# Scores of a pair of attention heads: full-row products replaced by half-row products, and all small-tile products of a pair in one run

## The chip, the cores and the metric

The program runs on one core of one Trainium2 chip. The core has five engines that work through their instructions in program order, each on its own: PE (TensorE, matrix products, with its weight loads shown apart as PEld), DVE (VectorE), ACT (ScalarE), POOL (GpSimd) and SP (SyncE, which here only issues DMA loads). They wait for one another through semaphores. Products are written to PSUM, which has eight banks; everything else lies in SBUF. The metric is the device time of one execution in microseconds (us).

## The reference

Two decoder layers on one sequence of 256 tokens with 1024 features. Layer 0 mixes tokens by dilated attention in 16 heads of 64 features, layer 1 by gated linear attention (GLA) in chunks of 64; each is followed by a gated ConvFFN. Shift, scale and gate of each sub-layer come from a vector c (`silu(c) @ w_ada`). The change is in the dilated attention:

```python
A_CONFIGS = ((128, 1), (512, 4), (2048, 16))       # (window, dilation), three groups g
qkv = (h @ w_in).reshape(B, S, A_GROUPS, 3, A_HEADS, A_HEAD_DIM)
for g, (window, dilation) in enumerate(A_CONFIGS):
    o, lse = dilated_branch(q[g] * scale, k[g], v[g], rel_bias[...], window, dilation)
# in a branch: query t attends keys t - j*dilation, j = 0..window/dilation
s = einsum('bnqrhe,bnkrhe->bnrhqk', qb, kk) + bias
s = where(mask, s, NEG_INF)
p = exp(s - max(s)); den = sum(p); o = p @ v / den; lse = max(s) + log(den)
# the three groups are mixed by their shares
wts = softmax(stack(lses), axis=0)
o = sum(wts[..., None] * stack(outs), axis=0)
y = o.reshape(B, S, A_WIDTH) @ w_out
```

Mixing three softmaxes by their log sums is one softmax over the keys of all three groups. The kernel works in that form: for each query one row of scores, 256 columns for group 0 (the "shared" scores: all tokens are possible keys) and 64 columns each for groups 1 and 2 (the "dilated" ones: only keys of the query's own residue modulo 4).

## The kernel before

**Products and weights.** Every large product is made in three passes of fp32r from a high and a low part of each operand (`mm3`, lines 175 to 177). `split` (L155) loads a piece of a weight on SP's queue into a slot `raw` (L159), ACT rounds it to `whi` (L165, two halves) and DVE subtracts to get `wlo` (L169, two halves). The slots `raw`, four of them, are shared with the pieces of `w_ada`, which `ada_chunk` loads (L133); DVE takes two products with c from each (L138) and ACT adds a bias (L146, L148). `next_ada()` is called once behind each of the three evacuations of a pair, and its load takes a `raw` slot too.

**Pairs of heads.** The attention works through eight pairs of heads, u = 0 to 7. For a pair, three pieces of 1 MB give q and k of the three groups (48 products each of 256 columns into a bank `pqk`), and two pieces of 0.75 MB give v (48 products of 384 columns into two banks `pv`). Pairs 0 and 1 get q and k from weights loaded at the very start. `evacuate` (L474 on) takes q and k out of PSUM: for groups 1 and 2 q on ACT (L479) and k on DVE (L480); for group 0 high and low parts of both, q into tiles in which the two heads stand on different rows with zeros elsewhere (L484, L485, written for each head apart), k (L489, L490). `by_group` (L494 on) copies v out: for the first 128 tokens on ACT (L497 to L500), for the second on DVE (L497, L498) and ACT (L499, L500). `pqk` and `pv` share two banks (tag `p`), so a pair's first pqk product has to wait until v of the pair before is copied.

**Scores.** `attend` goes over the four residues r of the query position. `shared` makes three products with all 128 rows of the array, where the zeros in q keep the heads apart: 64 queries of one head and 64 of the other in one tile (L417). `dilated` adds four products of 64x64 in two quadrants of the array (L424, two instructions of PE each). DVE adds the bias and takes the maximum (L435), ACT makes the exponentials (L444) with DVE's negated maximum (L441), DVE normalizes (L450, L451) to `pn`, PE transposes (L455), ACT or DVE copies to `pt` (L456), and the outputs are products with v (L460, L464) into a bank `po`, taken out at L469 and L470. The relative bias is a tile that is loaded from DRAM by four small DMAs a pair (L345, L346), once the loads issued before it stand in the queue.

**What sets the order.** Each engine runs in the order in which a scheduler has written out its instructions; it is fixed at build time, and it follows the pools (how many banks and slots there are) and `behind(...)`, which says that an instruction must stand after another on its engine. The banks have three tags: `p` 2, `s` 3, `t` 3. After the attention, `project` makes the output projection with w_out.

Of the kernel before, what the change touches and what calls it, by code (L numbers as in the profile page):

```python
# [18 lines left out]
P = 128  # L19
D = 1024  # L20
T = 256
# [36 lines left out]
def trunk(ctx: ExitStack, tc: tile.TileContext, I, out):  # L58
# [275 lines left out]
    shift(att, 32)  # L334
    rows = att.tile([16, NROW], F32, tag="pt", name="rows")

    def load_bias(u):

        b = att.tile([P, KEYS + 3], F32, tag="bias", name="bias")
        r = rows_d[:, :]
        for hh in range(2):
            own, at = slice(CH * hh, CH * hh + CH), r.offset + (2 * u + hh) * NROW
            nc.sync.dma_start(b[own, 2 * CH :], bass.AP(r.tensor, at, [[4, CH], [1, T + 3]]))  # L345
            nc.sync.dma_start(b[own, 0 : 2 * CH].rearrange("p (g x) -> p g x", g=2),  # L346
                              bass.AP(r.tensor, at + 512, [[1, CH], [P, 2], [1, CH]]))
        return b[:, :]
# [19 lines left out]
    with behind(norm_ops[0]):  # L368
        keep_warm(3)
        for i, (g, n) in enumerate(ROWS):  # L370
            c = slice(at, at + n)
            ps = bank("rows", "t")[:16, 0:n]
# [33 lines left out]
    def attend(u, q, k, v, bias):  # L406
# [3 lines left out]
        prob = [att.tile([P, KEYS + 3], F32, tag="prob", name="prob", bufs=6) for _ in range(4)]  # L410
        pt = att.tile([P, 4, KEYS], F32, tag="pt", name="pt")
        heads = [slice(E * hh, E * hh + E) for hh in range(2)]

        def shared(s, r):
            n = T + r + r % 2
            for i, (a, b) in enumerate(((0, 0), (1, 0), (0, 1))):
                mm(s[:, 0:n], q[0][a][:, r].rearrange("p a b -> p (a b)"), k[0][b][:, 0:n], start=(i == 0), stop=(i == 2))  # L417

        def dilated(s, r):
            own = slice(CH * r, CH * r + CH)  # L420
            for g in (1, 2):
                at = T + r + CH * (g - 1)
                for e in heads:
                    mm(s[e, at : at + CH], q[g][e, own], k[g][e, own], start=True, stop=True)  # L424

        for h in range(2):
            s = [bank("s", "s") for _ in range(2)]
            shared(s[0], 2 * h)
            dilated(s[0], 2 * h)
            shared(s[1], 2 * h + 1)  # L430
            dilated(s[1], 2 * h + 1)
            for i in range(2):
                r = 2 * h + i
                back = bass.AP(bias.tensor, bias.offset + KEYS - 1 + r, [bias.ap[0], [-1, KEYS + r]])
                nc.vector.tensor_tensor_reduce(  # L435
                    prob[r][:, 0 : KEYS + r], s[i][:, 0 : KEYS + r], back,
                    op0=ALU.add, op1=ALU.max, scale=1.0, scalar=-3e38, accum_out=m[:, r : r + 1],
                )
        for h in range(2):
            rs = slice(2 * h, 2 * h + 2)  # L440
            nc.vector.tensor_scalar(m[:, 4:8][:, rs], m[:, 0:4][:, rs], -1.0, None, op0=ALU.mult)  # L441
            for r in (2 * h, 2 * h + 1):
                c = prob[r][:, 0 : KEYS + r]
                nc.scalar.activation(c, c, AF.Exp, bias=m[:, 4 + r : 5 + r], accum_out=m[:, 8 + r : 9 + r])  # L444
            nc.vector.reciprocal(m[:, 12:16][:, rs], m[:, 8:12][:, rs])
            for r in (2 * h, 2 * h + 1):

                f = m[:, 12 + r : 13 + r]
                pn = att.tile([P, KEYS], F32, tag="pn", name="pn", bufs=3)
                nc.vector.tensor_scalar(grouped(pn[:, 0:T]), by_residue(prob[r][:, 0:T]), f, None, op0=ALU.mult)  # L450
                nc.vector.tensor_scalar(pn[:, T:KEYS], prob[r][:, T + r : KEYS + r], f, None, op0=ALU.mult)  # L451
# [4 lines left out]
                (nc.vector.tensor_copy if r % 2 else nc.scalar.copy)(pt[:, r, :], t[:, 0:KEYS])  # L456
        po = bank("po", "t")
        for n in range(2):
            for hh, e in enumerate(heads):
                mm(grouped(po[e, :T]), v[n][:, e], pt[:, :, P * n + E * hh : P * n + E * hh + E], start=(n == 0), stop=False)  # L460
        for r in range(4):
            for hh, e in enumerate(heads):
                at = P * (r % 2) + P + E * hh
                mm(po[e, CH * r : CH * r + CH], v[r // 2][:, at : at + E],  # L464
                   pt[:, r, T + E * hh : T + E * hh + E], start=False, stop=(r == 3))
# [8 lines left out]
    def evacuate(q, k, g, pq, pk):  # L474
# [7 lines left out]
        for hh in range(2):  # L482
            own = slice(E * hh, E * hh + E)
            nc.scalar.mul(qh[own, :, hh, :], grouped(pq[own]), 0.125)  # L484
            nc.vector.scalar_tensor_tensor(ql[own, :, hh, :], grouped(pq[own]), 0.125, qh[own, :, hh, :].bitcast(F32),  # L485
                                           op0=ALU.mult, op1=ALU.subtract)
# [15 lines left out]
    q_pair = [[att.tile([P, 4, 2, CH], F32R, tag=f"q0{i}{j}", name="q", bufs=1) for j in range(2)] for i in range(2)]  # L502
    for z in q_pair[0] + q_pair[1]:
# [576 lines left out]
```

## Time and profile before

| what | value |
|---|---|
| time of three runs | 786.73, 784.63, 786.98 us; median 786.73 |
| span of the profiled execution | 783.8 us |
| the profiled execution's own time | only the span is given; it lies 2.9 us below the median |
| PE, DVE, ACT, POOL busy | 771.8, 643.3, 481.6, 14.3 us |
| read from HBM | 182.59 MB, mean 236 GB/s by all queues |

The page gives for each engine the time in which it had an instruction running, and for a group of like instructions its line, engine, operation, output and inputs, how many, the busy time, the mean of one in ns, and the idle time of the engine just before with what ended it. In the timeline a row has start, duration, engine, line, operation, tiles, and how many; records of PE overlap, since products are pipelined. Times there are from the start of the span. The windows view gives the busy time of each engine in a stretch. SPq rows are DMA issues on SP's queue; a DMA's landing time is counted from its issue.

### The profile page before, as it was taken

Reading aid. Unit: us, or ns where it says so; the run is one execution under the profiler, and the core shown is the slowest. Engines: PE = TensorE matmul, PEld = TensorE weight load, DVE = VectorE, ACT = ScalarE, POOL = GpSimd, SP = SyncE. Lnnn points to the kernel's source line nnn. Section 1 sums busy time; section 2 is a strip of 40 time slices with the busy share of each in tenths; the row PEclk is TensorE's granted clock in tenths of the full one; section 3 lists DMA queues with packets and bytes.
Section 4 is the critical chain, followed back from the end, with each engine's and each line's share of the span. In section 5 each row is a group of like instructions: output and inputs, shape, how many; then the busy total and the mean of one; then the engine's idle time right before and its main releaser. Section 6 shows DMA issues by size and latency. Waiting matters only on the chain.

```text
span 783.8 us, 15888 instructions
## 1 busy us (share of the span) xinstructions
PE 771.8 (98%) x6416; PEld 743.3 (95%) x6416; DVE 643.3 (82%) x1160; ACT 481.6 (61%) x940; POOL 14.3 (2%) x40
## 2 busy tenths in 40 slices
PE   8999999999999999999999999999999999999997
PEld 5999989999999999999999999898999999999997
DVE  6998979878788758999998886797567898899762
ACT  5566555545545557866666655665667866667552
POOL 1000000000000010000000000000010000000000
PEclk9999999999999999999999999999999999999999
DMA  9998577595775726777645994966445765555651
GB/s 350 405 313 350 192 306 256 205 320 195 268 289 198 273 92 249 255 265 268 222 147 196 314 331 178 337 240 231 146 139 186 256 206 176 210 180 211 220 198 54
DMA packets 32616, 184.72 MB, mean 236 GB/s; under 512 B 5852, under 2 KB 7388, under 8 KB 16286
## 3 DMA queue, kind: packets, MB, share of 16 engines
q1 hardware_dynamic: 32160, 183.26, 65.6%
q8 instruction: 50, 0.82, 0.4%
q10 hardware_dynamic: 382, 0.45, 0.2%
q14 instruction: 24, 0.20, 0.1%
HBM read 182.59 MB, written 1.10 MB: 234 GB/s over the span
## 4 chain that ended last, share of the span: by engine, by line
PE 75%; DVE 12%; DMA 8%; ACT 3%; issue 2%; ACTq 0%; DVEq 0%
PE pab L176 10%; PE pab L177 10%; PE pab L175 10%; PE pd L175 5%; PE pd L176 5%; PE pd L177 5%; DVE wlo L169 5%; DMA raw<-in_wqk 4%; PE pqk L177 3%; PE pqk L176 3%; PE pqk L175 3%; DVE ada_raw L138 2%; PE py L175 2%; PE py L176 2%; DMA raw<-in_wv 2%; PE py L177 2%
## 5 line engine op out<-in xcount | busy, mean ns | idle before, releaser
L169 DVE TENSOR_TENSOR wlo<-raw,whi 128x1024 fp32r<-128x1024 f32 (+3 forms) x274 | 291.7, 1096 | 53.1 <-ACT whi L165 52.4
L165 ACT CAST whi<-raw 128x1024 fp32r<-128x1024 f32 (+3 forms) x274 | 245.5, 945 | 130.3 <-PE pab L176 40.6
L177 PE MATMUL pab<-hhi,wlo 128*128 128x256 f32 x672 | 184.7, 276 | 0.0
L176 PE MATMUL pab<-hlo,whi 128*128 128x256 f32 x672 | 184.6, 276 | 0.0
L175 PE MATMUL pab<-hhi,whi 128*128 128x256 f32 x672 | 183.2, 277 | 0.0
L176 PEld LDWEIGHTS pab<-hlo,whi 128*128 128x128 f32 x672 | 126.0, 188 | 0.2
L177 PEld LDWEIGHTS pab<-hhi,wlo 128*128 128x128 f32 x672 | 126.1, 188 | 0.0
L175 PEld LDWEIGHTS pab<-hhi,whi 128*128 128x128 f32 x672 | 125.1, 188 | 0.1
L138 DVE CUSTOM_DVE_ANT_0 ada_raw<-ada_raw,c_bc 128x1024 f32<-128x1024 f32 x96 | 113.4, 1218 | 12.4 <-DMA ada_raw<-in_w_ada 12.4
L176 PE MATMUL pqk<-hlo,whi 128*128 128x256 f32 x440 | 123.0, 284 | 0.3 <-DVE hlo L260 0.3
L177 PE MATMUL pqk<-hhi,wlo 128*128 128x256 f32 x440 | 122.4, 283 | 0.0
L175 PE MATMUL pqk<-hhi,whi 128*128 128x256 f32 x440 | 120.8, 286 | 0.5 <-ACT v L500 0.5
L177 PE MATMUL pd<-ghi,wlo 128*128 128x256 f32 x352 | 97.1, 276 | 0.0
L176 PE MATMUL pd<-glo,whi 128*128 128x256 f32 x352 | 97.1, 276 | 0.0
L175 PE MATMUL pd<-ghi,whi 128*128 128x256 f32 x352 | 96.8, 276 | 0.0
L176 PEld LDWEIGHTS pqk<-hlo,whi 128*128 128x128 f32 x440 | 83.6, 190 | 1.0 <-DVE hlo L260 0.5
L177 PEld LDWEIGHTS pqk<-hhi,wlo 128*128 128x128 f32 x440 | 83.2, 190 | 0.9 <-issue 0.7
L175 PEld LDWEIGHTS pqk<-hhi,whi 128*128 128x128 f32 x440 | 82.1, 191 | 1.7 <-ACT v L500 0.6
L176 PEld LDWEIGHTS pd<-glo,whi 128*128 128x128 f32 x352 | 66.1, 188 | 0.0
L177 PEld LDWEIGHTS pd<-ghi,wlo 128*128 128x128 f32 x352 | 66.1, 188 | 0.0
L175 PEld LDWEIGHTS pd<-ghi,whi 128*128 128x128 f32 x352 | 65.9, 188 | 0.0
L641 ACT ACTIVATE r<-pab,small 128x256 f32<-128x256 f32 x86 | 46.7, 559 | 15.5 <-DVE r L644 15.4
(215 smaller groups left out, 1307.2 us busy)
## 6 DMA issues: line engine op xcount, KB each, us to landing
ada_raw<-in_w_ada SPq DMA_DIRECT2D x47, 1024.0 KB, 6.6
raw<-in_w_up SPq DMA_DIRECT2D x42, 1024.0 KB, 5.0
raw<-in_w_down SPq DMA_DIRECT2D x32, 704.0 KB, 5.1
raw<-in_wqk SPq DMA_DIRECT2D x18, 1024.0 KB, 7.0
raw<-in_wv SPq DMA_DIRECT2D x14, 768.0 KB, 4.5
raw<-in_w SPq DMA_DIRECT2D x7, 960.0 KB, 6.5
raw<-in_w_out_a SPq DMA_DIRECT2D x4, 1024.0 KB, 6.2
raw<-in_w_v_b SPq DMA_DIRECT2D x4, 1024.0 KB, 6.7
```

The costliest lines, as they stand in the source:

```text
L138: nc.vector.tensor_tensor_reduce(w, w, c_bc, op0=ALU.mult, op1=ALU.add, scale=1.0, scalar=0.0, accum_out=dot,)
L165: copied[0] = nc.scalar.copy(hi[:, c], raw[:, c])
L169: last_lo[0] = nc.vector.tensor_tensor(lo[:, c], raw[:, c], hi[:, c].bitcast(F32), op=ALU.subtract)
L175: mm(ps, a[0], b[0], start=start, stop=False)
L176: mm(ps, a[0], b[1], start=False, stop=False)
L177: return mm(ps, a[1], b[0], start=False, stop=stop)
L641: nc.scalar.activation(r, u[:, :T], AF.Identity, scale=cw[2], bias=col(C_CB + 44 * l + f))
```

## The change

- **Shared scores.** `scores` (new) makes products on half the array's rows, K = 64: one head's features stand on rows 0 to 63, the other's on rows 64 to 127. A tile of scores holds 128 queries of one head (two residues), not 64 of each of two. There are twelve products of 256 or 258 columns (L419), the two heads in turn, each into a bank of its own: four banks. No zeros are needed in q, whose tiles are now 256 wide; `evacuate` splits q's group 0 with one instruction each (L489, L490).
- **Small products.** All sixteen 64x64 products of a pair stand in one run behind them, in all four quadrants (L426).
- **Outputs.** `outputs` of the pair before (L467, L471) stands right behind the scores of this pair, and the v products are cut in halves: the first half ahead of the scores, the second behind the outputs.
- **Bias.** A tile for each head, so eight DMAs a pair rather than four (L347, L348).
- **Banks.** `s` 4 and `t` 2 rather than 3 and 3, with another cycle of tags.

```diff
-    cycle = iter("pstpstst" * 1000)
+    cycle = iter("pstspsts" * 1000)
...
-        return psum.tile([P, 512], F32, tag=tag, name=name, bufs={"p": 2, "s": 3, "t": 3}[tag])
+        return psum.tile([P, 512], F32, tag=tag, name=name, bufs={"p": 2, "s": 4, "t": 2}[tag])
...
     def load_bias(u):
...
         for hh in range(2):
-            own, at = slice(CH * hh, CH * hh + CH), r.offset + (2 * u + hh) * NROW
-            nc.sync.dma_start(b[own, 2 * CH :], bass.AP(r.tensor, at, [[4, CH], [1, T + 3]]))
-            nc.sync.dma_start(b[own, 0 : 2 * CH].rearrange("p (g x) -> p g x", g=2), ...)
+            b = att.tile([P, KEYS + 2], F32, tag=f"bias{hh}", name="bias")
+            at = r.offset + (2 * u + hh) * NROW
+            for odd in range(2):
+                own = slice(CH * odd, CH * odd + CH)
+                nc.sync.dma_start(b[own, 2 * CH :], bass.AP(r.tensor, at + odd, [[4, CH], [1, T + 2]]))
+                nc.sync.dma_start(b[own, 0 : 2 * CH].rearrange("p (g x) -> p g x", g=2), ...)
...
-        def shared(s, r):
-            n = T + r + r % 2
-            for i, (a, b) in enumerate(((0, 0), (1, 0), (0, 1))):
-                mm(s[:, 0:n], q[0][a][:, r].rearrange("p a b -> p (a b)"), k[0][b][:, 0:n], start=(i == 0), stop=(i == 2))
-        def dilated(s, r):
-            own = slice(CH * r, CH * r + CH)
-            for g in (1, 2):
-                at = T + r + CH * (g - 1)
-                for e in heads:
-                    mm(s[e, at : at + CH], q[g][e, own], k[g][e, own], start=True, stop=True)
+    def scores(q, k):
+        s = [bank("s", "s") for _ in range(4)]
+        for h in range(2):
+            n = T + 2 * h
+            for i, (a, b) in enumerate(((0, 0), (1, 0), (0, 1))):
+                for hh, e in enumerate(heads):
+                    last = mm(s[2 * h + hh][:, 0:n], q[0][a][e, P * h : P * h + P], k[0][b][e, 0:n], start=(i == 0), stop=(i == 2))
+        own_keys = [(h, g, hh, odd) for h in range(2) for g in (1, 2) for hh, odd in ((0, 0), (1, 1), (0, 1), (1, 0))]
+        with behind(last):
+            for h, g, hh, odd in own_keys:
+                at = T + 2 * h + CH * (g - 1)
+                e, to = heads[hh], slice(CH * odd, CH * odd + CH)
+                own = slice(P * h + CH * odd, P * h + CH * odd + CH)
+                last = mm(s[2 * h + hh][to, at : at + CH], q[g][e, own], k[g][e, own], start=True, stop=True)
+        return s, last
...
-        for hh in range(2):
-            own = slice(E * hh, E * hh + E)
-            nc.scalar.mul(qh[own, :, hh, :], grouped(pq[own]), 0.125)
-            nc.vector.scalar_tensor_tensor(ql[own, :, hh, :], grouped(pq[own]), 0.125, ...)
+        nc.scalar.mul(qh, pq, 0.125)
+        nc.vector.scalar_tensor_tensor(ql, pq, 0.125, qh.bitcast(F32), op0=ALU.mult, op1=ALU.subtract)
...
+    for u in range(1, NPAIR):
+        bias = bias_of(u)
...
+            for g in range(u == 2, NG):
+                queries(u, g, q, k)
+            pv = [bank("pv", "p") for _ in range(2)]
+            end = values(u, 0, pv)
+        with behind(end):
+            s, last = scores(q, k)
+        with behind(last):
+            outputs(*waiting)
+            if u > 1:
+                values(u, 1, pv)
+        if u > 1:
+            v = by_groups(pv)
+        waiting = u, v, probabilities(s, bias)
+    outputs(*waiting)
```

`queries`, `values`, `by_groups` and `probabilities` hold what stood in the loop and in `attend` before. How the order moves, at three places:

PE, one pair, the scores: what stands there before (rows of another shape stand for products; pv of this pair, then pqk of the next pair):

```order
L177 MATMUL pv<-whi,hlo 128x384
L417 MATMUL s<-k,q 128x260 x3
L424 MATMUL s<-k,q 64x64 x4
L417 MATMUL s<-k,q 128x256 x3
L424 MATMUL s<-k,q 64x64 x4
L417 MATMUL s<-k,q 128x258 x3
L424 MATMUL s<-k,q 64x64 x4
L175 MATMUL pqk<-hhi,whi 128x256
```

And after the change, PE, the same place:

```order
L177 MATMUL pv<-whi,hlo 128x384
L419 MATMUL s<-k,q 128x256 x6
L419 MATMUL s<-k,q 128x258 x6
L426 MATMUL s<-k,q 64x64 x16
L467 MATMUL po<-pt,v 64x256 x4
L471 MATMUL po<-pt,v 64x64 x8
L175 MATMUL pv<-whi,hhi 128x384
```

The changes between the array's shapes are gathered, and the outputs of the pair before have moved up to the scores, between the two halves of the v products.

ACT, one pair, between the last q copy and the exponentials, before (`v<-pv` are the copies that free the banks `p`; the first `whi` rows are the next pair's first piece):

```order
L479 ACTIVATE q<-pqk 128x256
L165 CAST whi<-raw 128x1024 x2
L148 ACTIVATE mod<-dot,small 128x1
L146 ACTIVATE mod<-dot,one_b,small 128x1
L497 COPY v<-pv 64x256
L498 COPY v<-pv 64x2x128
L499 COPY v<-pv 64x128
L500 COPY v<-pv 64x128
L165 CAST whi<-raw 128x1024 x2
L499 COPY v<-pv 64x128
L500 COPY v<-pv 64x128
L444 ACTIVATE prob,m<-prob,m 128x384
```

And after the change, ACT, the same place:

```order
L486 ACTIVATE q<-pqk 128x256
L148 ACTIVATE mod<-dot,small 128x1
L146 ACTIVATE mod<-dot,one_b,small 128x1
L165 CAST whi<-raw 128x1024 x2
L476 CAST ohi<-po 128x256
L448 ACTIVATE prob,m<-prob,m 128x384 x2
L165 CAST whi<-raw 128x1024 x2
L448 ACTIVATE prob,m<-prob,m 128x386 x2
L501 COPY v<-pv 64x256
L502 COPY v<-pv 64x2x128
L503 COPY v<-pv 64x128
L504 COPY v<-pv 64x128
```

The v copies moved from ahead of the exponentials to behind all four, and the mods moved ahead of the `whi` of the next piece.

DVE, the same place, after the change (`ISA` with prob is the bias addition with maximum, L435 before; `wlo` is that of the next pair's first piece):

```order
L169 TENSOR_TENSOR wlo<-raw,whi 128x1024 x2
L439 ISA prob,m<-s,bias 128x384
L439 ISA m 128x1
L439 ISA prob,m<-s,bias 128x384
L439 ISA m 128x1
L439 ISA prob,m<-s,bias 128x386
L439 ISA m 128x1
L439 ISA prob,m<-s,bias 128x386
L439 ISA m 128x1
L445 TENSOR_SCALAR m<-m 128x2
```

All four stand in one run behind both halves of `wlo`; before, three stood there and the fourth behind the first normalization.

SP, the bias loads, before, between the v loads of a pair and the next pair's first piece:

```order
L159 DMA raw<-in_wv 128x1536 x2
L345 DMA bias<-rows_d 64x259
L346 DMA bias<-rows_d 64x2x64
L345 DMA bias<-rows_d 64x259
L346 DMA bias<-rows_d 64x2x64
L159 DMA raw<-in_wqk 128x2048
```

Four more stand there after the change, alternating L347 (64x258) and L348 (64x2x64), eight in all, and the first wqk load stands behind them.

More of the change, by code (lines that the diff above doesn't have):

```diff
@@ new lines, in trunk @@
+    bias = bias_of(0)
+    qk0, qk1 = new_qk(), new_qk()
+    for g in range(NG):
+        evacuate(*qk0, g, pqk0[2 * g], pqk0[2 * g + 1])
+    v = by_groups(pv)
+    for g in range(NG):
+        evacuate(*qk1, g, pqk1[2 * g], pqk1[2 * g + 1])
+    pv = [bank("pv", "p") for _ in range(2)]
+    with behind(values(1, 0, pv)):
+        s, last = scores(*qk0)
+    with behind(last):
+        values(1, 1, pv)
+    waiting = 0, v, probabilities(s, bias)
+    v = by_groups(pv)
+    for n in range(2):
+        next_ada()
```

180 lines of the change are left out of this document (89 added, 91 removed).

## The prediction

> **What bounds the kernel now.** I read the page first: the busy shares, the chain that ended last, and the groups.
>
> ```profile
> span 783.8 us, 15888 instructions
> PE 771.8 (98%) x6416; PEld 743.3 (95%) x6416; DVE 643.3 (82%) x1160; ACT 481.6 (61%) x940; POOL 14.3 (2%) x40
> PE 75%; DVE 12%; DMA 8%; ACT 3%; issue 2%; ACTq 0%; DVEq 0%
> ...
> L175 PE MATMUL pqk<-hhi,whi 128*128 128x256 f32 x440 | 120.8, 286 | 0.5 <-ACT v L500 0.5
> ```
>
> PE works 98% of the span, so the whole program reads as bound by products. But a quarter of the chain lies on other engines, and the last row names one of the few places where PE waits: its first pqk product of a pair waits for a copy of v out of PSUM, 0.5 us in all. Next the windows view, one stretch for each pair of heads from po block to po block (start:end, length, busy us of PE, PEld, DVE, ACT, POOL; the other two stretches are 31.93 and 31.32 long), with its closing row, which gives the means:
>
> ```profile
> 158.42:190.12 31.70, 31.70 (x273) 30.40 (x272) 24.94 (x52) 17.82 (x41) 0.20 (x2) 1.00 0.69 241
> ...
> sum 94.95, PE 94.95 PEld 90.78 DVE 76.69 ACT 52.28 POOL 0.41; mean PE 31.65 PEld 30.26 DVE 25.56 ACT 17.43 POOL 0.14
> ```
>
> A pair takes 31.65 us and PE is busy in all of it, at full clock. DVE has 6.1 us free, ACT 14.2. So before, PE sets a pair's time, and anything saved on PE arrives, until something else takes 31.65 us to go round. That is the question of this change.
>
> **What PE saves.** The timeline of PE (start, duration, engine, line; records overlap, so a cost is the distance between starts):
>
> ```profile
> 71.66 0.62 PE L417 MATMUL s<-k,q 128*128 128x256 f32 x3
> 72.21 0.45 PE L424 MATMUL s<-k,q 64*64 64x64 f32 x8
> 72.59 0.63 PE L417 MATMUL s<-k,q 128*128 128x258 f32 x3
> ...
> 191.04 0.63 PE L464 MATMUL po<-pt,v 128*64 128x64 f32 x16
> 191.60 0.38 PE L176 MATMUL pqk<-hlo,whi 128*128 128x256 f32 x1
> ...
> 192.29 0.28 PE L175 MATMUL pqk<-hhi,whi 128*128 128x256 f32 x1
> ...
> 194.22 0.28 PE L177 MATMUL pqk<-hhi,wlo 128*128 128x256 f32 x1
> ...
> 211.85 0.49 PE L455 MATMUL t<-ident,pn 128*128 128x128 f32 x3
> 212.10 0.36 PE L175 MATMUL pqk<-hhi,whi 128*128 128x256 f32 x1
> 212.30 0.49 PE L455 MATMUL t<-ident,pn 128*128 128x128 f32 x3
> ```
>
> From 192.29 to 194.22 lie 17 products of 256 columns: 0.1135 us each. One residue's scores take 72.59 - 71.66 = 0.93: three products (0.34), eight small ones of 64x64, and two changes of the array's tile shape. The po tail takes 191.60 - 191.04 = 0.56: sixteen small ones and one change back. Taking the small ones as equal in both, 0.59 = 8a + 2s and 0.56 = 16a + s give a = 0.022 and s = 0.21 us a change. Three transposes cost 212.30 - 211.85 less a product, 0.34.
>
> Changes of shape: before, two in each of four residues and two round po, ten a pair. Now the twelve shared products, the sixteen 64x64 ones and po stand in a row: 128 to 64 rows, to 64x64, to 128x64, and back, four. Six fewer, 6 x 0.21 = 1.25 us. Shared scores: twelve full products before (1.36 us), twelve on half the rows now. Whether two halves run at once, no score of before shows; the GLA's state products, on rows 0 to 63 and 64 to 127, do:
>
> ```profile
> 522.08 0.48 PE L825 MATMUL kv<-v,kdT 64*128 64x256 f32 x1
> 522.08 0.48 PE L825 MATMUL kdt<-v,kdT 64*128 64x256 f32 x1
> ```
>
> Both start at 522.08. So six slots of 0.1135 replace twelve: -0.68; bounds -0.68 and 0, and I take the overlap. The small products fill four quadrants rather than two: 32 x 0.022 = 0.70 to 0.35, -0.35; bounds -0.35 and 0, taken as overlapping like the halves. Output products keep their number and sizes: 0. PE needs 1.25 + 0.68 + 0.35 = 2.3 us a pair less, 29.35; with no overlap at all 30.4. For eight pairs that is 18 us, or 10.
>
> **What the others pay, and where it goes round.** Less work: q's two parts come from one 128-row instruction each rather than two, some 0.4 on ACT and 0.4 on DVE a pair, and POOL's clearing of q is gone (POOL is idle). More work: four bias loads on SP's queue. Moved: on ACT the copies of v stood ahead of the exponentials and now stand behind all four; on DVE the four bias additions with maximum (L435, now L439) stand together behind both wlo halves of the next pair's first wqk piece; scores no longer straddle the first products of the next pair. The rows (ACT and DVE in groups and timeline, then SP):
>
> ```profile
> L165 ACT CAST whi<-raw 128x1024 fp32r<-128x1024 f32 (+1 forms) x30 | 27.4, 961 | 27.6 <-DMA raw<-in_wv 16.8 <-DMA raw<-in_wqk 10.8
> L479 ACT ACTIVATE q<-pqk 128x256 f32<-128x256 f32 x6 | 2.3, 375 | 0.0
> L500 ACT COPY v<-pv 64x128 f32<-64x128 f32 x6 | 1.6, 263 | 0.1
> L499 ACT COPY v<-pv 64x128 f32<-64x128 f32 x6 | 1.6, 258 | 3.5 <-DVE v L498 3.5
> L498 ACT COPY v<-pv 64x256 f32<-64x256 f32 x3 | 1.1, 369 | 0.0
> L497 ACT COPY v<-pv 64x256 f32<-64x256 f32 x3 | 1.0, 350 | 0.0
> ```
>
> ```profile
> 208.72 0.62 ACT L444 ACTIVATE prob<-prob,m 128x384 f32<-128x384 f32 x1 [2.31 <-DVE m L441]
> ...
> 209.94 1.99 ACT L165 CAST whi<-raw 128x1024 fp32r<-128x1024 f32 x2
> ```
>
> ```profile
> L169 DVE TENSOR_TENSOR wlo<-raw,whi 128x1024 fp32r<-128x1024 f32 (+1 forms) x30 | 32.8, 1114 | 12.4 <-ACT whi L165 12.3
> L480 DVE COPY k<-pqk 128x256 f32<-128x256 f32 x5 | 2.1, 414 | 0.0
> ```
>
> ```profile
> 207.09 0.56 DVE L435 CUSTOM_DVE_ANT_0 prob<-s,bias 128x384 f32<-128x384 f32 x1
> ...
> 208.53 0.16 DVE L441 TENSOR_SCALAR m<-m 128x2 f32<-128x2 f32 x1
> ...
> 217.36 1.22 DVE L138 CUSTOM_DVE_ANT_0 ada_raw<-ada_raw,c_bc 128x1024 f32<-128x1024 f32 x1
> ...
> 219.65 0.95 DVE L169 TENSOR_TENSOR wlo<-raw,whi 128x768 fp32r<-128x768 f32 x1
> ```
>
> ```profile
> 219.76 0.33 SPq L159 DMA_DIRECT2D raw<-in_wv  x1
> 220.14 0.45 SPq L345 DMA_DIRECT2D bias<-rows_d  x1
> ...
> 221.28 0.60 SPq L345 DMA_DIRECT2D bias<-rows_d  x1
> ```
>
> ```profile
> raw<-in_wv SPq DMA_DIRECT2D x1, 768.0 KB, 5.0
> ```
>
> ```profile
> ada_raw<-in_w_ada SPq DMA_DIRECT2D x1, 1024.0 KB, 5.0
> ```
>
> Each engine works in the order shown in the section on the change, so a pair closes a loop, from PE's first pqk product to the next pair's. First loop: 144 pqk products (16.34), six transposes (0.68), the last one's drain (0.28 - 0.11 = 0.17); q on ACT 0.38; k on DVE 0.41; the two ada products of that piece, 217.36 to 219.65, 2.29; their mod on ACT, taken like q, 0.38; first whi half 0.96; two wlo 2.2; four bias additions at (208.53 - 207.09) / 3 = 0.48, 1.92; m 0.16; two exponentials 208.72 to 209.94, 1.22; whi of the next piece 1.92; two exponentials 1.22; the four v copies 0.35 + 0.37 + 0.26 + 0.26 = 1.24. Only then is the bank free that the next pqk product writes. Sum 31.5 us. Twelve hand-offs come on top; m ends at 208.69 and ACT starts at 208.72, so 0.03 at the least, and 0.1 as my upper estimate: 31.9 to 32.7. PE's scores, outputs and v products, that is all that the change makes faster, are not in this loop: they run beside DVE and ACT.
>
> Second loop, through SP: second wv issue 0.38; eight bias issues at (221.28 - 220.14) / 2 = 0.57, 4.56, then 0.6 more because in the built program the eighth waits for that wv load, which lands after 5.0 (seven issues are over at 0.38 + 4.0); the first wqk piece lands 5.0 later (a 1 MB load alone); whi, wlo, bias additions, m, exponentials, whi, exponentials, v copies as above 10.84; the first 48 pqk products with six transposes and drain 6.3; q and k in two parts on ACT and DVE 1.6; ada 2.29, which frees the slot that the second wv load waits for. Sum 31.6, with fourteen hand-offs 32.0 to 33.0. Before, four bias issues fewer make it 2.3 + 0.6 shorter, and v copies ahead of the exponentials shorten both; so PE's 31.65 was the longest.
>
> I take 32.5 us a pair, the middle of the two: 0.85 more than 31.65 at the seven boundaries from pair 1 on, +6.0. PE then waits 32.5 - 29.35, some 3 us a pair, for the v copy. The first pair has no such loop: PE's saving against a later start of its scores, bounds -2.3 and +3, taken as 0. Before the last v products PE waited like this:
>
> ```profile
> 263.02 0.33 PE L424 MATMUL s<-k,q 64*64 64x64 f32 x4
> 263.99 0.45 PE L175 MATMUL pv<-whi,hhi 128*128 128x384 f32 x1 [0.63 <-DVE k L480]
> ```
>
> Now the last k copy stands behind two wlo of the output projection on DVE: 2 x 1.11 = 2.2 at most, 0 at the least if DVE is ahead; taken 1.5, since PE's own lateness hides little there. After the attention nothing changes but bank names: 0. Sum +7.5 us: 783.8 to 791.3 in the profiled execution, which lies 2.9 below the median, hence 794.2 against 786.73.
>
> **The rivals.** *The saving arrives* (faster, the other side): the loops close under 29.35 and PE stays the bound, 786.7 - 18 = 769, or 777 without overlap. For it: PE 98%, DVE 25.56 and ACT 17.43 of 31.65, and a v wait of 0.5 us over the whole run. Against it: the two sums. It decides at 31.65: the v copies would have to come 0.85 us earlier for a gain at all and 3 us for all of it, as with an earlier wqk load and exponentials ahead of the whi. By the totals no copy out of PSUM is a bottleneck and the sum is 769; by the order it is 794. [...]
>
> *The saving turns into waits of its own size*: hand-offs at their least and scores that let DVE start sooner give 31.65 a pair, 786.7 within 2.4 us.
>
> *Halves and quadrants do not overlap*, so the change doesn't do what it says: PE needs 30.4, still under 32.5, and the time stays 794; only the wait shrinks, to 2 us. This is a share of the main case.
>
> *The queue jams.* The same 1 MB load takes 8.4 us when it queues behind others:
>
> ```profile
> ada_raw<-in_w_ada SPq DMA_DIRECT2D x1, 1024.0 KB, 8.4
> ```
>
> If the first wqk piece meets that each pair, the second loop grows by 3.4: from 805 (half of the seven pairs) to 817. Against it: it is issued behind small bias loads and a landed wv load. [...]
>
> **How the numbers follow.** The forecast, loops of 32 to 33 us a pair with the bounds of the first pair and the tail, 789 to 801: 0.65. Saving arrives, 769 to 784: 0.12. Cancels within 2.4: 0.15. Jam: 0.08. Within 0.3% (2.4 us) a measurement of this kernel can't tell a change. The range leaves out the first and the last rival: 784 to 802. Faster 0.12, same 0.15, slower 0.73.
>
> **What would show it.** Right: a wait of 2 to 3 us in PE ahead of the first pqk product (L175) of each pair, ended by ACT's v copy (L504); stretches from po to po of 32 to 33 us; PE busy some 18 us less in all; the halves of L419 starting together; scores with no product between. Wrong: no such wait and stretches of about 29.4 (saving arrives), the wait ended by the wqk load and a landing above 8 us (jam), or halves that start 0.11 apart (no overlap). Most doubtful is the loop's closing time: 1 us less a pair turns the sign.

## The result and the profile after

The changed kernel takes 807.11 us (median of four runs, 804.1 to 810.67) against 786.01 for the kernel before in the same job: ratio 1.0272, 95% interval 1.0234 to 1.0311. It is slower by 21 us, where +7.5 was forecast, and outside the range (784 to 802). The profiled execution (804.60 us by its own time) spans 802.8 us, 19.0 more than before. The page after:

```profile
span 802.8 us, 15908 instructions
PE 766.5 (95%) x6416; PEld 737.7 (92%) x6416; DVE 642.1 (80%) x1152; ACT 481.6 (60%) x932; POOL 12.4 (2%) x36
PE 69%; DVE 12%; DMA 10%; ACT 5%; issue 2%; SPq 2%; ACTq 0%; DVEq 0%
...
L175 PE MATMUL pqk<-hhi,whi 128*128 128x256 f32 x440 | 123.7, 293 | 13.4 <-ACT v L504 9.6
```

PE is busy 5.3 us less, where 18 were forecast, and for 95% of the span instead of 98%; the v copy that ended 0.5 us of waiting before now ends 9.6. The waits view of PE over the attention (60 to 330 us; total, times, longest):

```profile
PE pqk L175 <- ACT v L504: 9.6, 4, 2.4
PE t L459 <- DVE pn L454: 6.1, 7, 2.0
PE pv L175 <- DVE k L487: 4.0, 1, 4.0
PE t L459 <- DVE pt L460: 2.3, 1, 2.3
```

Four waits of 2.4 us at the place that the prediction named; 6.1 us at transposes for normalized probabilities (`pn`), 3.6 of it before 116.28 us, and 2.3 more there for a copy of transposed ones (`pt`); 4.0 us ahead of the last v products. In stretches from one pair's first pqk product to the next (start:end, length, busy us of PE, PEld, DVE, ACT, POOL, granted clock, DMA share, GB/s), first after, then before:

```profile
74.40:116.28 41.88, 37.92 (x353) 34.58 (x353) 34.01 (x73) 23.49 (x52) 0.40 (x4) 0.93 0.78 273
116.28:149.10 32.82, 30.31 (x275) 28.96 (x273) 26.18 (x52) 18.32 (x41) 0.20 (x2) 1.00 0.68 249
149.10:182.12 33.02, 29.89 (x273) 28.34 (x273) 25.89 (x52) 18.18 (x41) 0.20 (x2) 1.00 0.69 252
182.12:216.92 34.80, 31.54 (x272) 29.98 (x272) 25.95 (x52) 17.81 (x39) 0.20 (x2) 0.94 0.65 238
...
251.65:290.93 39.28, 34.43 (x272) 32.51 (x273) 26.43 (x54) 17.73 (x38) 0.00 (x0) 0.88 0.57 201
290.93:315.21 24.28, 24.28 (x223) 23.80 (x224) 14.31 (x25) 13.83 (x27) 2.39 (x2) 1.00 0.36 128
```

```profile
73.53:109.99 36.46, 36.01 (x323) 33.47 (x320) 31.07 (x67) 21.52 (x46) 0.23 (x2) 1.00 0.72 256
...
141.48:172.98 31.50, 31.50 (x276) 30.19 (x272) 25.60 (x52) 17.54 (x41) 0.20 (x2) 1.00 0.72 255
...
236.13:268.85 32.72, 32.09 (x277) 30.35 (x273) 27.00 (x54) 18.30 (x40) 0.00 (x0) 1.00 0.70 249
268.85:296.87 28.02, 26.82 (x243) 25.92 (x240) 19.76 (x44) 16.04 (x35) 2.39 (x2) 1.00 0.37 130
```

The account: +0.9 until the first of these stretches and +5.4 in it; +1.4 on average in the next two, whose clock is full; +3.2 in each of the two whose clock is 0.94 (34.80, and 34.73 for the one not shown, against 31.66 and 31.49); +6.6 in the last pair, of which 3.7 come back in the stretch behind it, since less of the scores is left there. Together +18.3 of the 19.0.

In the two stretches with full clock PE works 30.31 and 29.89 us, near the 29.35 of the sum, and is idle for the rest. The run of scores costs what was forecast: from 170.49 to 171.40 twelve half-row products with a change of shape (0.91; forecast 0.68 + 0.21), then 0.62 to the first output product at 172.02 (forecast 0.35 + 0.21):

```profile
170.49 0.98 PE L419 MATMUL s<-k,q 64*128 64x256 f32 x12
171.40 0.69 PE L426 MATMUL s<-k,q 64*64 64x64 f32 x32
```

And the chain that ended last goes, pair after pair, through the second loop, with no PE work but the first pqk products in it (start, duration, what):

```profile
159.69 5.22 DMA raw<-in_wv
164.93 0.60 SPq L348
165.63 5.36 DMA raw<-in_wqk
171.01 1.05 ACT whi L165
172.09 2.36 DVE wlo L169 x2
174.45 0.47 DVE prob L439
...
176.48 1.31 ACT prob L448 x4
177.79 1.88 ACT whi L165 x2
179.67 1.21 ACT prob L448 x4
180.89 0.25 ACT v L501
...
181.80 0.27 ACT v L504
182.12 0.40 PE pqk L175
```

The eighth bias load (L348) waits for the v piece to land, the wqk piece is issued behind it, whi, wlo, bias additions, exponentials and v copies follow, and then PE starts at 182.12. The other boundaries are alike: there the first wqk piece lands 5.35, 5.51 and 5.09 us after its issue. Two things were not in the sum. The first is the clock: PE's products behind that wait are 0.21 us apart instead of 0.1135, while the granted clock is 0.50, for 3.41 us (PE's busy time stands third, the clock third from the end):

```profile
178.95:182.36 3.41, 0.89 (x7) 0.56 (x6) 3.37 (x6) 3.35 (x10) 0.00 (x0) 1.00 0.39 161
182.36:185.77 3.41, 3.41 (x18) 3.41 (x18) 3.34 (x9) 2.62 (x5) 0.00 (x0) 0.50 0.66 223
```

These slow products lie on the chain: from the first of them to the q copy it takes 8.08 us (182.12 to 190.20) and at the next boundary 7.86, against 6.45 behind 149.10, where the clock is 1.00.

The second is the start. Sixteen bias loads, where eight stood before, stand ahead of the first wqk piece, which is issued at 66.24 us; before, at 56.30 (SP's queue, after and before). The last of the sixteen starts 3.1 us after the one ahead of it has been issued, so their issue times alone are not the whole delay:

```profile
61.98 0.45 SPq L347 DMA_DIRECT2D bias<-rows_d  x1
65.54 0.60 SPq L348 DMA_DIRECT2D bias<-rows_d  x1
66.24 0.54 SPq L159 DMA_DIRECT2D raw<-in_wqk  x1
```

```profile
56.30 0.38 SPq L159 DMA_DIRECT2D raw<-in_wqk  x1
```

### The profile page after: what moved, and what is told of

The parts are those of the page before. It is cut to its first block, busy times and chain, and to the rows that moved or that the text cites. A ratio compares the mean times of both kernels' runs of the same rounds, so it can differ in the third digit from the quotient of the medians.

```text
span 802.8 us, 15908 instructions
## 1 busy us (share of the span) xinstructions
PE 766.5 (95%) x6416; PEld 737.7 (92%) x6416; DVE 642.1 (80%) x1152; ACT 481.6 (60%) x932; POOL 12.4 (2%) x36
## 4 chain that ended last, share of the span: by engine, by line
PE 69%; DVE 12%; DMA 10%; ACT 5%; issue 2%; SPq 2%; ACTq 0%; DVEq 0%
PE pab L175 10%; PE pab L176 10%; PE pab L177 10%; PE pd L175 5%; PE pd L177 5%; PE pd L176 5%; DVE wlo L169 5%; DVE ada_raw L138 3%; DMA raw<-in_wv 3%; DMA raw<-in_wqk 3%; PE pqk L175 2%; DMA ada_raw<-in_w_ada 2%; PE pqk L177 2%; PE pqk L176 2%; ACT whi L165 2%; PE py L175 2%
## 5 line engine op out<-in xcount | busy, mean ns | idle before, releaser
L175 PE MATMUL pqk<-hhi,whi 128*128 128x256 f32 x440 | 123.7, 293 | 13.4 <-ACT v L504 9.6
L176 PE MATMUL pqk<-hlo,whi 128*128 128x256 f32 x440 | 125.1, 288 | 0.0
L177 PE MATMUL pqk<-hhi,wlo 128*128 128x256 f32 x440 | 124.5, 287 | 0.0
L175 PEld LDWEIGHTS pqk<-hhi,whi 128*128 128x128 f32 x440 | 85.4, 198 | 15.5 <-ACT v L504 10.6
L177 PEld LDWEIGHTS pqk<-hhi,wlo 128*128 128x128 f32 x440 | 86.6, 197 | 0.7 <-DVE wlo L169 0.3
L176 PEld LDWEIGHTS pqk<-hlo,whi 128*128 128x128 f32 x440 | 86.7, 197 | 0.1
```

The lines of the kernel that those rows point to most:

```text
L175: mm(ps, a[0], b[0], start=start, stop=False)
L176: mm(ps, a[0], b[1], start=False, stop=False)
L177: return mm(ps, a[1], b[0], start=False, stop=stop)
```

## The experiments

Theory A is that the products do save their time and the order loses it: copies that free PE's banks stand, on engines that work in order, behind something that waits for the next pair's first wqk piece. The rivals are B (the clock is a sign, not a cause), C (the loads themselves bind) and D (the new tiles save nothing). All ratios are to the kernel before in the same job. Diffs are to the changed kernel.

**e1_warm: filling the wait.**

```diff
             if u > 1:
-                values(u, 1, pv)
+                end = values(u, 1, pv)
         if u > 1:
+            with behind(end):
+                keep_warm(8, "s")
```

> The changed kernel with eight idle products (no part of the result) written into PE's order behind the second half of the v products of pairs 2 to 7, so that they fill most of the 2.4 us wait for the v copies; nothing else moved. Theory A (the wait lets the granted clock fall, and the slow products then lengthen the loop): the clock stays above 0.95 at the first pqk products of pairs 4 to 7 (0.56, 0.52 and 0.50 now), the distances between them fall from 34.8 to about 33.0, time about 6 us less, 801. Rival B (those products were slow because operands came late; the clock is a sign, not a cause): distances and time stay, 807 or up to 2 more.

803.12 us, ratio 1.0213 (1.0183 to 1.0242): by the medians 4 us less than the changed kernel, not 6, and the single runs of the two touch (800.22 to 804.61 against 804.1 to 810.67). Of the middle pairs one slow stretch was left (clock 0.84 at 182.5 to 184.5). Filling the wait is worth little; what of it is the clock, e12 takes up.

**e2_vfirst: exponentials behind the v copies.**

```diff
+                with behind(*(last_v if late else ())):
                     nc.scalar.activation(c, c, AF.Exp, ...)
```

> The changed kernel with the exponentials of pairs 2 to 7 written behind the copies of v on ACT, as they stood before the change; loads, banks and PE's order but for transposes stay. Theory A (both loops run through the exponentials because the v copies stand behind them): PE's wait for the v copy falls from 2.4 us to under 1.8, the clock stays up from pair 3 on, time 778 to 784. Rival C (the eight bias loads on SP's queue hold the first wqk piece, wherever the v copies stand): that piece still lands as late, PE then waits for its parts instead, time 800 or more.

793.95 us, 1.0099 (1.0065 to 1.0133): 13 us less, but neither number. PE's waits at the v copy, which A had falling, come to 11.6 us in five, the longest 3.6; some half of the gain lies in the last pair (33.3 us to the output projection, not 39.3), where the wait for the k copy is gone. The chain shows why the v copy is still late:

```profile
166.30 9.66 DMA raw<-in_wqk
...
175.99 1.99 ACT whi L165 x2
177.97 0.27 ACT v L504
...
179.22 0.39 PE pqk L175
```

The exponentials are out of the loop, but the v copies still stand behind whi of a piece that lands 9.66 us after its issue. So part of A and part of C hold: the copy is late because of its place in line, and what stands ahead of it is late because of the load.

**e3_bias: bias loads a pair earlier.**

```diff
             pv = [bank("pv", "p") for _ in range(2)]
+            if u + 1 < NPAIR:
+                soon[u + 1] = bias_of(u + 1)
             end = values(u, 0, pv)
```

> The changed kernel with a pair's bias loads issued a pair earlier, ahead of the v loads, so that the first wqk piece stands right behind the v loads; ACT's order stays as the scheduler makes it. Rival C (the bias loads on the queue are what holds the loop): distances of 30 to 31, clock up, 785 to 790. Theory A (two loops of nearly the same length, one without the queue): the distances stay 32 or more with PE waiting at another place (k or v copies behind wlo and exponentials), 795 to 808.

810.79 us, 1.0310 (1.0279 to 1.0341), no faster than the changed kernel. With the wqk load no longer behind the bias loads, the scheduler wrote wlo of that piece ahead of the last k copy on DVE, and PE waited there (waits view of PE over the attention):

```profile
PE pv L175 <- DVE k L487: 12.9, 6, 4.2
```

That is A's mechanism (the wait moves to the k copy); the time is 2.8 us above its range.

**e4_straight: v products not cut round the scores.**

```diff
-        with behind(end):
-            s, last = scores(q, k)
-        with behind(last):
-            outputs(*waiting)
-            if u > 1:
-                values(u, 1, pv)
+        if u > 1:
+            values(u, 1, pv)
+        outputs(*waiting)
+        s, last = scores(q, k)
```

> The changed kernel with the same products, tiles, banks and bias loads, but in the loop the v products are no longer cut in halves round the scores: both halves, then the outputs of the pair before, then the scores; the scheduler places them. Theory A (the products do save some 2 us a pair, the order loses it): v copies stand ahead of the exponentials again, no wait above 1 us from pair 2 on, clock above 0.99, 774 to 781. Rival D (half-row and quadrant products save nothing): 786 or more.

783.70 us, 0.9977 (0.9963 to 0.9991): 23 us less than the changed kernel, with the same products, tiles, banks and loads, and 0.2% faster than before. So the order lost the time. The time is only 2.3 us under D's line of 786, so what the tiles are worth is read from e8. It gained less than expected: in this build the run of scores and outputs is torn apart again, and pairs take 31.0 us with PE busy all the time, in all but the first of five stretches.

It says something of the start too. The same sixteen bias loads stand ahead of the first wqk piece, which is issued at 65.35 us, and yet the first stretch, which took 41.88 us in the changed kernel and 36.46 before, takes

```profile
73.52:110.76 37.24, 35.68 (x303) 32.88 (x303) 28.19 (x53) 19.16 (x42) 0.20 (x2) 0.91 0.76 271
```

The late piece alone doesn't make the long start, then; the changed kernel's order has a part in it.

**e5_block: the run kept whole behind both halves of v.**

```diff
+        if u > 1:
+            end = values(u, 1, pv)
         with behind(end):
             s, last = scores(q, k)
         with behind(last):
             outputs(*waiting)
-            if u > 1:
-                values(u, 1, pv)
```

> The changed kernel with both halves of the v products ahead of the scores, and scores, small products and the outputs of the pair before kept as one run behind them (the fourth experiment's order, but the run is not torn apart; loads and banks as in the changed kernel). Theory A (only the place of the v products and their copies lost the time): v is copied while PE makes the run, some 3.0 us, so PE's first pqk product waits under 0.5 us; the clock stays up; a pair takes 29.4 to 30.4 us rather than 31.0 as in the fourth experiment, time 770 to 776. Rival C (bias loads on the queue): the first wqk piece lands late here too, PE waits for its parts 2 us a pair or more, 785 or more.

781.99 us, 0.9939 (0.9914 to 0.9964). No wait at the v copy is left, and a pair takes 29.38 to 30.81 us, 30.0 on average: three of five stretches as expected, two 0.3 and 0.4 us above, with PE waiting for wlo of the v piece. The shortest:

```profile
236.14:265.52 29.38, 29.38 (x276) 28.57 (x273) 25.96 (x49) 19.62 (x38) 0.00 (x0) 1.00 0.80 291
```

PE alone needs 29.38 us here, and 29.63 on average of the five; the sum had 29.35. The total missed its 770 to 776, by the start in the main: the first of the stretches begins at 76.04, behind idle times of 2.8 and 0.8 us, and is still 39.4 us long (to 115.41), with 2.2 us idle in it.

**e6_both: e2 and e3 together.**

> The second and third experiment together: exponentials behind the v copies, and the bias loads a pair earlier. Theory A as it stands after them (in the third the wait moved to the k copy, which stands on DVE behind the parts of a wqk piece that lands late; in the second to the v copies, which stand on ACT behind whi of such a piece): the wait at the k copy stays, since the wlo of the next pair's first piece stand ahead of it on DVE, 794 to 806. Rival C (each half alone fails only because the other remains): 778 to 786.

812.47 us, 1.0336 (1.0309 to 1.0363). The wait at the k copy was there as A said (17.4 us in six waits), and the time was 6 us above the expectation. The two edits do not add up; rival C in the form that each hides the other falls.

**e7_same: heads one after another.**

```diff
-            for i, (a, b) in enumerate(((0, 0), (1, 0), (0, 1))):
-                for hh, e in enumerate(heads):
+            for hh, e in enumerate(heads):
+                for i, (a, b) in enumerate(((0, 0), (1, 0), (0, 1))):
```

> The fifth experiment with the shared products of one head written one after another, three and three, so that neighbours use the same half of the array's rows and no two run at once. If halves do run at once (a slot of 0.076 us each, switch included, in the changed kernel): the twelve take about 1.5 us rather than 0.9, and 0.6 us more a pair, 4 us in all where PE is the bound, 774 to 780. If they don't: no difference from the fifth, within 0.2%.

782.05 us, 0.9939 (0.9922 to 0.9955): no difference from e5. But not because the halves don't overlap. In this build's order three products of one half stand ahead of three of the other (but in the first pair), and still the twelve take 0.92 us, from 204.29 to 205.21, or 0.077 each with a change of shape, where a full-row product takes 0.1135:

```profile
204.29 0.99 PE L419 MATMUL s<-k,q 64*128 64x256 f32 x12
205.21 0.51 PE L426 MATMUL s<-k,q 64*64 64x64 f32 x18
```

In e5 (202.42 to 203.33) and in the changed kernel they take 0.91. So the expectation's premise, that neighbours in the order must be on different halves, fell, and its reading of "no difference" with it. The price without overlap was not measured.

**e8_full: new order, old tiles.** Scores, bias loads (four a pair) and output products of the kernel before, in e5's order:

```diff
+        for r in range(4):
+            n = T + r + r % 2
+            for i, (a, b) in enumerate(((0, 0), (1, 0), (0, 1))):
+                last = mm(s[r][:, 0:n], q[0][a][:, r].rearrange(...), k[0][b][:, 0:n], ...)
+        with behind(last):
+            for r in range(4):
+                ...
```

> The order of the fifth experiment with the scores, tiles, bias loads (four a pair) and output products of the kernel before: full rows with zeros in q, 64 queries of each head a tile; but the twelve shared products stand together and the sixteen small ones in one run behind them. It tells the new order from the new tiles. If the tiles are worth what the prediction says (0.68 for half rows, 0.35 for quadrants): about 1 us a pair slower than the fifth, 776 to 782. If the order and the gathering give it all: the same as the fifth, within 2 us.

779.97 us, 0.9921 (0.9905 to 0.9938), no slower than e5. Its run costs more:

```profile
196.85 1.59 PE L413 MATMUL s<-k,q 128*128 128x256 f32 x12
198.36 1.15 PE L420 MATMUL s<-k,q 64*64 64x64 f32 x32
```

1.51 and 1.08 us to the next start, against 0.91 and 0.62: the tiles are worth 1.06 us a pair (the sum had 0.68 + 0.35), and pairs take 31.1 us on average against 30.0 in e5. But it starts 8 us earlier (its second pqk stretch begins at 107.53, e5's at 115.41), with twelve bias loads at the start rather than 24. The total can't tell the two; the stretches can, and so D falls by PE's own time (30.76 us busy in a stretch of e8, 29.63 of e5). In the total, the new order with the old tiles does as well as order and tiles together.

**e9_three: e6 and wlo of the next first piece behind the last k copy (DVE). e10_threelater: the same, bias loads behind a pair's own wqk pieces. e13_q: e10, and whi of that piece behind the last q copy (ACT).**

```diff
-        w = split(I["wqk"][u - 2, g], 2048)
+        w = split(I["wqk"][u - 2, g], 2048, low=last_k[-1:] * (g == 0), late=last_k[-1:] * (g == 0),
+                  after=[last_q[-1:] * (g == 0)] * 2)          # this line in e13 alone
```

> The sixth experiment (exponentials behind the v copies, bias loads a pair earlier) with one constraint more: on DVE the wlo parts of a pair's first wqk piece stand behind the last k copy of the pair before, as in the changed kernel before the loads were moved. Theory A (each engine's order puts something that waits for the first wqk piece ahead of a copy that frees PE's banks; the products are sound): the 3 us waits at the k copy go, PE waits about 0.8 us at the v copy only, distances 30 to 31 us, no slow clock from pair 2 on, 778 to 788, some 25 to 30 less than the sixth. Rival C (what is left is the queue and its loads): waits of 2 us or more remain at another place, 795 or more.

> The ninth experiment, but each pair's bias loads are issued in its own turn, behind its wqk pieces and ahead of its v pieces, so that at the start sixteen small loads no longer stand ahead of the second wqk piece. If the start of the changed kernel is late because of those loads (that piece is issued at 66 us there, at 56 us before): PE's first waits of 2 and 1.3 us shrink and pair 2 starts about 5 us earlier, 774 to 782, 3 to 6 less than the ninth. If not: the same as the ninth within 2 us.

> The tenth experiment with one constraint more, on ACT: whi of a pair's first wqk piece stands behind the last q copy of the pair before. Theory A (whatever waits for the late piece and stands ahead of a copy that frees PE's bank is the wait): PE's waits of 2 to 4 us at the first v product go, distances fall from 33 to 35 to about 31, 776 to 786. Theory C (the piece lands late, and its consumers are late wherever they stand): the wait moves to the first pqk products, distances stay above 32.5, 792 or more.

e9 gave 804.80 us, 1.0253 (1.0221 to 1.0285), a miss: by its own line rival C. The chain shows the same thing once more on another engine: whi of the late piece stands ahead of the q copy on ACT.

```profile
197.01 7.07 DMA raw<-in_wqk
...
204.16 1.99 ACT whi L165 x2
206.16 0.29 ACT q L487
...
206.47 0.43 DVE k L488
...
206.95 0.44 PE pv L175
```

e10: 799.39 us, 1.0188 (1.0157 to 1.0220), 5.4 less than e9, and the second stretch starts at 112.42 instead of 116.55: moving the loads is worth what was expected in this order, though the total wasn't near its 774 to 782. (What the expectation calls the second wqk piece is the first on SP's queue.) e13, with the ACT order alone changed against e10: 789.30 us, 1.0054 (1.0033 to 1.0074), another 10 us less. The waits at the first v product are gone but in two places and distances are 30.75 to 32.02 us; 7.6 us in six waits for the v copy stay, as in e10. It is 3 us above A's upper end and on A's side of C's line; the last pair still waits 4.3 us, for the same reason with the output projection's weights.

**e11_best: e5 with e10's bias loads and e9's constraint. e15_blockq: with e13's too.**

> The fifth experiment (scores, small products and outputs as one run behind both halves of the v products) with the two steps of the last two: bias loads behind a pair's wqk pieces, and wlo of the next first piece behind the last k copy. Theory A: PE is the bound in all pairs, 29.4 to 30 us each, and the start is 5 us earlier than in the fifth: 770 to 777, the fastest here. Rival (with PE that fast the loads or DVE take over): distances above 30.5, 778 or more.

> The eleventh experiment with the same constraint on ACT. Theory A: waits at the first v product (1.2 to 2.3 us in every second pair) go, distances 29.5 to 30.5, 772 to 779. Theory C: PE waits for whi or wlo of the first piece instead, 783 or more.

787.88 us, 1.0033 (1.0016 to 1.0049), and 784.92, 0.9999 (0.9981 to 1.0016): the constraint on ACT again takes the waits at the v products away (6.3 us in e11, 0.3 in e15), but both miss and neither beats e5. Both reach the second pqk stretch early (108.31 and 108.91 us, e5 115.41) and lose it again in pairs of 30 to 34 us. In e15 PE waits 5.6 us at transposes for normalized probabilities instead. Why these come later in it than in e5 isn't settled.

**e12_warmall: more filler.** Ten idle products ahead of each v wait, twelve in the first pair's wait, sixteen in the last one's.

> The first experiment with more idle products (no part of the result): ten instead of eight ahead of each v wait, twelve in the first pair's wait and sixteen in the last pair's wait for the k copy. Theory A (the slow clock behind waits costs about 10 us of the changed kernel, of which the first experiment got 4 back): no stretch of pqk or pv products at half speed is left, mean clock 0.995 or more, 794 to 800. Rival B (the clock costs little beyond what the first experiment showed): 802 or more.

803.32 us, 1.0232 (1.0203 to 1.0262): B's branch. The mean clock is back at 0.993 (0.981 in the changed kernel, 0.998 before) and all four middle stretches show 1.00, yet they are no shorter than in the changed kernel: 135.4 us together in both, 133.3 in e1. The longest:

```profile
183.59:218.98 35.39, 32.35 (x292) 31.13 (x293) 26.06 (x52) 17.29 (x39) 0.20 (x2) 1.00 0.65 234
```

With 2.4 us of filler inside, PE is busy 32.35 us, so 30 without it: the faster products wait for a loop. It is another loop than the changed kernel's: the chain goes through DVE's normalizations, a v piece, the bias issues and the wqk piece, with no PE work in it. So the experiment shows that filling brings some 4 us, not the 10 that the slow products suggest; what the clock costs in the changed kernel's own order, where the chain does pass through them, it doesn't show.

**e16_blockless: e5 with half of the w_ada traffic.**

```diff
-            ada_chunk(*rest.pop(0))
+            ada_chunk(*rest.pop(0), cols=1024)
```

> The fifth experiment with half of each w_ada piece loaded in the attention (both dot products are made from the first half, so modulation values differ and 1.5 MB a pair of traffic is gone; DVE and ACT do as much as before). Theory C (loads bind what the orders don't): distances fall below 29.6, the start's waits of 2.8 and 2.2 us shrink, 770 to 776 against 782. Theory A (orders and PE bind): the pairs stay at 29.5 to 30.5 and only the start can gain, 777 to 782.

790.24 us, 1.0068 (1.0047 to 1.0089), slower than e5, outside both branches. The scheduler wrote another order for it (PE waits 5.2 us for the first v copies). With the order moved it can't tell whether loads bind e5's pairs; that stays open.

## Why the prediction was wrong

- **PE's saving.** Nearly right: 29.35 us a pair forecast; in e5, where little else binds, PE is busy for 29.38 to 29.83, 29.63 on average. The run of scores came out at 0.91 and 0.62 us, forecast 0.89 and 0.56, and the halves do start together (two by two in the changed kernel's run, the first two at 170.49). But PE is busy only 5.3 us less in all, not 18: between 60 and 330 us the granted clock is 0.50 for 23.9 us, and half of that, at most 12 us by my estimate, can be busy time that the clock added.
- **The loops.** Right in place and nearly in size: PE waits 2.40 us for the v copy (forecast "2 to 3"), the chain is the second loop step by step, and the stretches with full clock take 32.82 and 33.02 us (forecast 32 to 33, taken 32.5). With the same products in another order the loss is gone: e4 and e5.
- **The copies out of PSUM.** By the totals none was a bottleneck; by the order the v copy became one: 9.6 us of PE's waiting ends with it, where 0.5 did before. It is a copy's place in line, not ACT's load: ACT is busy for the same 481.6 us as before.
- **"The first pair has no such loop: ... bounds -2.3 and +3, taken as 0"** is the first step that failed: up to the end of that stretch the changed kernel is 6.3 us behind. I counted four more small loads a pair as queue time in the loop, and not that at the start sixteen of them stand ahead of the first wqk piece, which was issued 10 us later, nor that PE would wait 5.9 us there at transposes. Moving the loads gave 5.4 us in one order (e10 against e9); another order of PE gave 4.6 of the stretch's 5.4 back with the loads left where they were (e4). So the late piece and the order seem to have made it together, and how much is owed to each in the changed kernel is open.
- **The clock** is the second; the sum has no term for it. Behind three of the four waits of 2.4 us, those that end at 182.12, 216.92 and 251.65, the granted clock is 0.50; behind the one that ends at 149.10 it is 1.00. The two middle stretches with slow products are 1.8 us longer than the two without (3.2 against 1.4 over before), and 1.6 and 1.4 of that is seen on the chain, between the first pqk product and the q copy. Filling the waits gave some 4 us back in all, by way of another loop.
- **The last pair**: the wait ahead of the last v products was taken as 1.5, 2.2 at most, and is 4.0. The k copy stood behind wlo, as said, but also behind the load that wlo waits for, which landed after 7.11 us:

```profile
266.68 7.11 DMA raw<-in_w_out_a
...
273.89 1.05 ACT whi L165
274.97 1.26 DVE wlo L169 x2
...
277.25 0.43 DVE k L487
```

- **The range.** The time lies where the jam rival had put it (805 to 817; its own working, 794.2 and 3.4 for half or all of seven boundaries, gives 806 to 818), and that is luck for it: in the chain the first wqk piece lands after 5.1 to 5.5 us, near the 5.0 of my sum, not after 8.4.

By place, measured against forecast: the start +6.3 for 0.85 (one boundary); the four middle stretches +9.2 for 4 x 0.85 = 3.4, of which 3.6 goes with the slow clock and the rest is a loop 0.55 longer than taken; the last pair and what follows +2.8 for 1.5 and two boundaries, 3.2, so that the longer wait there is made up elsewhere. The start and the middle are off by about the same, 5.4 and 5.8. What remains open is why e11 and e15, with most of the waits that had been named out of the way, don't go below e5.

## What to carry to other kernels

When PE is made faster, write down each engine's order from one reuse of a bank to the next and sum it: a loop that PE's own work hid before becomes the bound, and busy shares of 60% and 80% don't show it. On an engine that works in order, let nothing that waits for a load stand ahead of a copy that frees a bank. Constraint by constraint the wait mostly moved on (k copy on DVE, v copy on ACT, q copy on ACT), while one change of PE's own order, v products not cut round the scores, took 23 to 25 us back at once (e4, e5). And sum the start and the tail with the same care as the steady stretch, with each small DMA in the queue counted there.

## What the runs showed of the hardware

- Two tiles on different halves of the array's rows ran side by side even where the order has three products of one half ahead of three of the other: in e7 the twelve take 0.92 us, in e5 and in the changed kernel 0.91, while twelve full-row products take 1.51 in e8.
- The granted clock of the changed kernel between 60 and 330 us is 0.50 in five stretches, 23.9 us together: 6.83 us each from 73.13 and from 250.62, 3.41 us each from 182.36, 216.49 and 277.93. In the 3.41 us ahead of 182.36 (shown with the result) PE is idle for 2.52 us. Ahead of 149.10 it waits just as long as ahead of 182.12, 2.40 us, but is idle for 1.65 us in the 3.41 us up to 148.23 and for 0.87 in the 3.41 behind, and the clock stays at 1.00:

```profile
144.82:148.23 3.41, 1.76 (x12) 1.23 (x10) 3.33 (x9) 3.40 (x8) 0.00 (x0) 1.00 0.67 281
```

No run was made to tell how much idle time brings the lower clock.
- A change of tile shape came to about 0.21 us, an estimate from the two equations of the prediction (0.59 = 8a + 2s and 0.56 = 16a + s, from the timeline of before); the two runs of products that it went into came out 0.02 and 0.06 us above their sums (0.91 and 0.62 us, forecast 0.89 and 0.56).
